# GpSimd's long products in pieces, retention's decay in the addition, and five weight buffers in place of four

## The chip, the cores and the metric

The kernel runs on one core of one Trainium2 chip. What counts is the device time of one execution, in microseconds, as the median of several runs. TensorE (PE in the profile) multiplies matrices, PEld is its loading of weights, VectorE is DVE, ScalarE is ACT, GpSimd is POOL, and SP (SyncE) issues the DMAs.

## What is computed

One inference step of a two-layer decoder trunk of width 2048, for 272 positions of a prompt and 8 sequences of 4 new tokens, 304 columns together. In each layer one input projection feeds four mixers (gated delta, RG-LRU, GLA, retention); their outputs are gated and go through one output projection. The reference, cut to the projections and to retention, whose state update the change touches:

```python
proj = jnp.einsum('bld,de->ble', rms_norm(x, lp['norm']), lp['w_in'])
(qkv_a, alpha_a, beta_a, x_b, q_c, k_c, v_c, r_c, q_d, k_d, v_d, gate) = split_last(proj, IN_SIZES)
...
def step(s, inp):                      # retention, one chunk; S_t = gamma_h S_{t-1} + k_t^T v_t
    qc, kc, vc = inp
    attn = jnp.einsum('bihk,bjhk->bhij', qc, kc) * intra
    o = (jnp.einsum('bihk,hi,bhkv->bihv', qc, from_state, s)
         + jnp.einsum('bhij,bjhv->bihv', attn, vc))
    s_new = s * chunk_decay[:, None, None] + jnp.einsum('bjhk,hj,bjhv->bhkv', kc, to_state, vc)
    return s_new, o
...
mixed = jnp.concatenate([o_a, o_b, o_c, o_d], axis=-1) * jax.nn.silu(gate)
y = x + jnp.einsum('ble,ed->bld', mixed, lp['w_out'])
```

Delta and GLA have the same form of update: the old state times a decay, plus a product of keys and values.

## The kernel before

All activations lie transposed: 128 features in the partitions, the 304 columns in the free dimension. The weights of a projection are cut into units of 4 blocks of 128x128. A unit is loaded by one DMA of 256 KB into a buffer `raw`; ScalarE rounds it to `hi` (a type that TensorE multiplies fast), VectorE subtracts to get the rest `lo` from `raw` and `hi`, and TensorE then does 12 matrix products with it: `hi` with the high and the low part of the activations (`xh`, `xl`), and `lo` with the high part, for each of the 4 blocks. There are 512 units, so 6144 of these products, which the profile lists as `main` (in the start also as `d`). `RB` and `HB` are the numbers of `raw` and of `hi`/`lo` buffers, and they also set how far ahead the steps stand: at the start of unit u the program has `low(u + HB - 2)`, `split(u + HB - 1)` and, behind the second block, `load(u + HB - 2 + RB)`.

Between these products the mixers' small work is woven in. Each mixer is a generator (`delta_thread`, `pair_thread` for GLA with m = "g" and retention with m = "r", `lru_thread`), and a clock model in the program, with a price for each kind of instruction, decides behind which product the next piece of a generator is written. So the order on each engine is fixed when the program is built, and every engine works strictly in its own order. A small product whose input is late on the chip holds up all products behind it. The tag `e` names the PSUM banks of rows, GLA, LRU and retention, `d` those of delta.

The states of the 8 new-token sequences and of the prompt lie in one tile `S9` of 9 blocks of 128x128. A mixer reads the old state with 9 small products (`reads`, whose left side `lxd`, `lxg` or `lxr` is copied together by GpSimd), GpSimd multiplies the state by its decay, and later VectorE adds new products (`advance`). For these GpSimd spreads the values over the sequences (`spread`): 8 blocks in one instruction for delta, twice 4 for GLA and retention. `o_norm` sums squares by two products with ones, whose two inputs are `hq` (ScalarE) and `lq` (VectorE). `zq` and `zk` are the inputs of GLA's level products. The line L302 is that of the helper that records every instruction.

Of the kernel before, what the change touches and what calls it, by code (L numbers as in the profile page):

```python
# [9 lines left out]
F32 = mybir.dt.float32  # L10
# [34 lines left out]


KU = 4
HB = 4
RB = 4
NH = KT // KU  # L50
NW = 16
NN = 20
# [301 lines left out]
def trunk(ctx: ExitStack, tc: tile.TileContext, I, O):  # L354
    nc = tc.nc
    clk = Clocks()
    pe, act, dve, pool, sp = (Engine(e, k, clk) for e, k in ((nc.tensor, "P"), (nc.scalar, "A"), (nc.vector, "V"),
                                                             (nc.gpsimd, "G"), (nc.sync, "S")))
    mul, add, sub = ALU.mult, ALU.add, ALU.subtract
# [17 lines left out]
    def store(out, in_):  # L377
        r = clk.ready
        sp.dma_start(out=out, in_=in_)
        clk.ready = r  # L380
# [30 lines left out]
    def C(name, a=0, n=1):  # L411
        return cst[:, CC[name] + a:CC[name] + a + n]
# [22 lines left out]
    els = one.tile([128, 12], F32, name="els")  # L435
# [110 lines left out]
    def spin(t, tag, n):  # L546
        turn[tag] = (turn.get(tag, -1) + 1) % n
        clk.slot[t.tensor.name] = f"{tag}{turn[tag]}"
        return t
# [15 lines left out]
    def load(u, to=KU):  # L565
# [3 lines left out]
        if u == 0:  # L569
            if u not in raws:  # L570
                raws[u] = spin(wp.tile([128, KU, 128], F32, tag="raw", name="raw", bufs=RB), "raw", RB)
            k = 0 if to < KU else 1
            store(raws[u][:, k:to, :], I["w_in"][l, e - 1][:, k:to, :])
            return
        raws[u] = spin(wp.tile([128, KU, 128], F32, tag="raw", name="raw", bufs=RB), "raw", RB)
        store(raws[u], (I["w_in"][l, e - 1] if ph == "in" else I["w_out"][l, e])[:, KU * q:KU * q + KU, :])

    def split(u):
        if u >= len(units):
            return  # L580
        r = raws.pop(u)
        his[u] = spin(wp.tile([128, KU, 128], F32R, tag="hi", name="hi", bufs=HB), "hi", HB)
        los[u] = spin(wp.tile([128, KU, 128], F32R, tag="lo", name="lo", bufs=HB), "lo", HB)
        for ks in PARTS if u == 0 else (slice(0, KU),):
# [259 lines left out]

    def spread(vm, R, blocks):

        n = blocks.shape[1]
        pool.tensor_mul(vm, R[:, None, 128:256].bitcast(F32).to_broadcast([128, n, 128]),
                        blocks[:, :, None].to_broadcast([128, n, 128]))

    def copies(out, x, n):

# [2 lines left out]
            pool.tensor_copy(out=out[:, 128 * b:128 * b + 16 * n].rearrange("p (u t) -> p u t", u=n),  # L855
                             in_=x[:, None, c:c + 16].to_broadcast([128, n, 16]))

    def advance(tag, S9, p0, n, products):
        ps = pt(tag)
        for i, (out, k, v) in enumerate(products):  # L860
            pe.matmul(ps[out, :128 * n], k, v, start=i == 0 or out.start > 0,
                      stop=i + 1 == len(products) or products[i + 1][0].start > 0)
        dve.tensor_add(S9[:, p0:p0 + n, :], S9[:, p0:p0 + n, :],
                       ps[:, :128 * n].rearrange("p (b v) -> p b v", v=128))

    busy = []

# [31 lines left out]
    def delta_thread(l, p, tag):  # L899
# [4 lines left out]
        K, Q, V, KN, VB, KTL, Eb, AT, qe, egl = ({} for _ in range(10))  # L904
# [16 lines left out]
        for h in range(2):  # L921
            ps = yield from totals(tag, s[h][:, :T])
# [15 lines left out]
        for h in range(2):  # L938
            for src, d, k in ((V, VB, 1), (KN, KTL, 3)):
                d[h] = yield from take(1, src is V)  # L940
                ps = pt(tag)
# [49 lines left out]
        for r in range(2):  # L991
            for u in range(2):
                n = 512 - 16 * u
# [4 lines left out]
        for j in range(15):  # L998
            n, m = 15 - j, j // 2 + 1
# [39 lines left out]
        for h, c, a in hca:  # L1039
            r = slice(32 * a, 32 * a + 32)  # L1040
# [6 lines left out]
        for h, c, a in hca:  # L1047
            r = slice(32 * a, 32 * a + 32)
# [53 lines left out]
        VN, SS, S9 = {}, {}, {}  # L1102
# [7 lines left out]
        ps = pt(tag)  # L1110
# [5 lines left out]
        ps = pt(tag)  # L1116
# [5 lines left out]
        ps = pt(tag)  # L1122
        for h in range(2):
            pe.matmul(ch(ps, h), KN[h][:, 128:256], SS[h][:, 0:128], start=True, stop=True)
        for h in range(2):
            dve.scalar_tensor_tensor(ch(VB[h], 1), ch(ps, h), col[:, 2, 1, hs[h]:hs[h] + 1], ch(VB[h], 1),
                                     op0=mul, op1=add)
        yield
        ps = pt(tag)
# [5 lines left out]
        ps = pt(tag)  # L1135
# [5 lines left out]
        LQ, SL, R = {}, {}, {}  # L1141
# [5 lines left out]
        ps = pt(tag)  # L1147
# [4 lines left out]
        for h in range(2):  # L1152
            R[h], LQ[h] = yield from take(2)
            R[h] = recast(R[h], F32R)
            pk = pt(tag)
            pe.transpose(pk[:, 0:128], KN[h][:, 256:384], ident)
            pool.memset(LQ[h][:, 0:128], 0.0)
            sc = col[:, 3, 2, hs[h]:hs[h] + 1]
            hi_lo(R[h][:, 0:128], pk[:, 0:128], 64, sc)
            activ(LQ[h][0:16, 0:128], pk[0:16, 0:128], AF.Copy, scale=sc[0:16])  # L1160
            spots(lx["d"], 0, slice(0, 128), KN[h])
            spots(lx["d"], 1, slice(0, 128), qe[h])
            give(KN[h])
            yield
            pr = reads(tag, lx["d"], S9[h])
            activ(SL[h][:, 0:128], pr, AF.Copy)
            pool.tensor_mul(S9[h], S9[h], egl[h][:, 2:11, None].to_broadcast([128, 9, 128]))
            yield
        for h in range(2):
            ps = pt(tag)  # L1170
# [6 lines left out]
        for h in range(2):  # L1177
# [4 lines left out]
            ps = pt(tag)  # L1182
# [14 lines left out]
        for h in range(2):  # L1197
            vm = recast((yield from take9()), F32R)
# [84 lines left out]
    def pair_thread(l, p, m, tag):  # L1283
# [23 lines left out]
        S9 = yield from take9()  # L1307
# [44 lines left out]
        if m == "r":  # L1352
            yield from bg.vacant(tag, 2)
            ps2 = [pt(tag), pt(tag)]
            for c, (c0, n) in enumerate(CH):
                for h in range(2):
                    r = slice(64 * h, 64 * h + 64)
# [5 lines left out]
        for h in range(2):  # L1363
            ps = pt(tag)
# [82 lines left out]
        R = yield from take(2)  # L1447
        R = [recast(x, F32R) for x in R]
        ps, ps2 = pt(tag), pt(tag)
# [9 lines left out]
        else:  # L1459
            for h in range(2):  # L1460
                for c in range(2):
                    b = 128 * c + 64 * h
# [4 lines left out]
        for b in range(2):  # L1467
            hm = C("hs", 0, 2)[:, :, None].to_broadcast([128, 2, 64])
            v, k = ps2[:, 128 * b:128 * b + 128], ps2[:, 256 + 128 * b:384 + 128 * b]
# [5 lines left out]
            for h in range(2):  # L1475
                r, own = slice(64 * h + 32, 64 * h + 64), slice(64 * h, 64 * h + 64)
                if sc is None:
                    dve.tensor_sub(R[b][r, own], k[r, own], R[b][r, own].bitcast(F32))
                else:
                    dve.scalar_tensor_tensor(R[b][r, own], k[r, own], sc[r], R[b][r, own].bitcast(F32),  # L1480
                                             op0=mul, op1=sub)
            activ(R[b][:, 128:256], v, AF.Copy)
            dve.scalar_tensor_tensor(R[b][:, 128:256], R[b][:, 128:256].bitcast(F32), C("um", 0), v,
                                     op0=mul, op1=add)
# [7 lines left out]
        ps = pt(tag)  # L1492
        for c in range(2):
            for h in range(2):
                b = 128 * c + 64 * h
# [10 lines left out]
        pr = reads(tag, lx[m], S9)  # L1506
        activ(sel[:, 0:128], pr, AF.Copy)
        if m == "g":
            pool.tensor_mul(S9, S9, els[:, 2:11, None].to_broadcast([128, 9, 128]))
        else:  # L1510
            pool.tensor_scalar(S9[:, 0, :], S9[:, 0, :], C("dec", 3 * p + 1), None, op0=mul)
            pool.tensor_scalar(S9[:, 1:9, :], S9[:, 1:9, :], C("dec", 3 * p + 2), None, op0=mul)
        yield
        sqs_ = yield from take(2)
        yield from bg.vacant(tag, 2)
        ps = [pt(tag), pt(tag)]
        for h in range(2):
            r = slice(64 * h, 64 * h + 64)
# [9 lines left out]
        for h in range(2):  # L1528
# [3 lines left out]
            give(sqs_[h])  # L1532
        give(sel, SS, qe)
        advance(tag, S9, 0, 1, [(slice(64 * h, 64 * h + 64), ktb[:, 64 * h:64 * h + 64], VT[h][0:16, 256:384])
                                for h in range(2)])
        give(*VT)
        vm = recast((yield from take9()), F32R)
        for b in range(2):
            spread(vm[:, 4 * b:4 * b + 4], R[b], C("m4", 0, 4))
        yield  # L1540
        for b in range(2):
            advance(tag, S9, 1 + 4 * b, 4, [(slice(0, 128), R[b][:, 0:128], vm[:, 4 * b:4 * b + 4, :])])
            yield
        give9(recast(vm, F32))
        give(*[recast(x, F32) for x in R])
# [91 lines left out]
    load_x(2, 2)  # L1637
    for u in range(1, RB):
        load(u)
# [9 lines left out]
    for kt in range(KU):  # L1649
        x_split(0, kt, xin[kt])  # L1650
        if kt < HB - 1:
            split(kt)
            if kt < HB - 2:
                low(kt)
                load(kt + RB)
    for kt in range(LAG):
        squares(kt, xin[kt], sqs[kt % 6])

    def begin(u):
        kt = KU + u  # L1660
        if kt < KT:
            x_split(0, kt, xin[kt])
        low(u + HB - 2)
        split(u + HB - 1)
        load(u + HB - 2 + RB)
        for k in range(LAG + u, KT) if kt == KT else (LAG + u,):
# [47 lines left out]
    for u, (l, ph, e, q) in enumerate(units):  # L1714
# [4 lines left out]
        else:  # L1719
            low(u + HB - 2)  # L1720
            split(u + HB - 1)
            if LOADK == 0:
                load(u + HB - 2 + RB)
        if ph == "in" and q == 0:
# [20 lines left out]
        a, b = ([t[:, k, :] for k in range(KT)] for t in (xh, xl)) if ph == "in" else (mh, ml)  # L1745
# [21 lines left out]
        if q == NH - 1:  # L1767
# [4 lines left out]
            kind, i = ORDER[e]  # L1772
# [109 lines left out]
```

## Time and profile before

| what | before |
|---|---|
| median of 3 runs | 1091.02 us (1091.01 to 1096.0) |
| profiled execution: time, span of the instructions | 1089.9 us, 1088.0 us |
| mean granted TensorE clock | 0.991 |
| TensorE products: busy | 1042.6 us, 96% |
| VectorE, ScalarE, GpSimd: busy | 746.0, 639.7, 412.9 us |
| DMA | 186.86 MB, mean 172 GB/s |

The busy time of TensorE counts a product from its start to its modelled end, and products overlap in the pipeline; so the small difference between busy time and span is idle time, while a product that comes late by less than the pipeline's depth does not show as idle. The last TensorE product ends some 9 us before the span's end.

### The profile page before, as it was taken

The numbers are of one execution on the slowest core, as the hardware profiler recorded it, in microseconds if no ns is written. First come the engines' busy times: TensorE is split into PE (matmuls) and PEld (weight loads), VectorE is DVE, ScalarE is ACT, GpSimd is POOL, SyncE is SP. The second block draws the span as 40 slices with busy tenths as digits, with TensorE's granted clock in tenths as the row PEclk, the third lists the DMA queues.
The fourth block names the chain that finished last, engine by engine and source line by source line (L and its number), as shares of the span: only waits on it lengthen the run. The fifth ranks groups of instructions, "written<-read, shape, count | busy, mean of one in ns | idle before, by whom it ended". The sixth has DMA issues, their size and how long they took to land.

```text
span 1088.0 us, 23535 instructions
## 1 busy us (share of the span) xinstructions
PE 1042.6 (96%) x8358; PEld 995.1 (91%) x8358; DVE 746.0 (69%) x1457; ACT 639.7 (59%) x1438; POOL 412.9 (38%) x843
## 2 busy tenths in 40 slices
PE   8999999998999999999999998999999999899995
PEld 7899988988998999999999998888999998899995
DVE  5867588798656467556667757878886576765664
ACT  6677954665745766455455876555765466554542
POOL 4423374534518343022222348344254346211110
PEclk9999999999999999999999999999999999999998
DMA  6555434545465555666644545336545663566563
GB/s 212 188 150 187 134 123 138 189 148 190 139 208 186 174 165 181 198 208 211 206 134 144 178 149 164 126 102 212 178 152 159 201 214 122 176 202 207 184 191 138
DMA packets 116893, 186.86 MB, mean 172 GB/s; under 512 B 22184, under 2 KB 45368, under 8 KB 116776
## 3 DMA queue, kind: packets, MB, share of 16 engines
q1 hardware_dynamic: 116776, 185.37, 53.1%
q8 instruction: 65, 1.06, 0.4%
q14 instruction: 52, 0.43, 0.1%
HBM read 164.10 MB, written 19.96 MB: 169 GB/s over the span
## 4 chain that ended last, share of the span: by engine, by line
PE 67%; DVE 13%; DMA 5%; POOL 5%; issue 5%; ACT 4%; SPq 1%; DVEq 0%; ACTq 0%; POOLq 0%
PE main L302 55%; PE e L302 6%; PE d L302 5%; DMA raw<-in_w_in_dram 4%; DVE lo L302 4%; DVE m L302 2%; DVE n L302 2%; POOL m L302 2%; ACT hi L302 1%; DVE zq L302 1%; DVE acc L302 1%; POOL s9.4_4198 L302 1%; POOL n L302 1%; ACT L369 1%; SPq L302 1%
## 5 line engine op out<-in xcount | busy, mean ns | idle before, releaser
L302 PE MATMUL main<-xh,hi 128*128 128x304 f32 (+2 forms) x1488 | 468.7, 315 | 2.8 <-ACT xh L302 2.5
L302 DVE TENSOR_TENSOR lo<-raw,hi 128x512 fp32r<-128x512 f32 (+1 forms) x513 | 391.7, 782 | 101.6 <-ACT hi L302 100.0
L302 PE MATMUL main<-xh,lo 128*128 128x304 f32 (+2 forms) x1488 | 449.8, 302 | 4.2 <-DVE lo L302 4.2
L302 ACT ACTIVATE hi<-raw 128x512 fp32r<-128x512 f32 (+1 forms) x513 | 316.7, 625 | 228.6 <-PE main L302 95.9
L302 PE MATMUL main<-xl,hi 128*128 128x304 f32 (+2 forms) x1488 | 447.6, 301 | 0.4 <-DVE xl L302 0.3
L302 PEld LDWEIGHTS main<-xh,hi 128*128 128x128 f32 x1488 | 281.8, 189 | 14.8 <-issue 6.8
L302 PEld LDWEIGHTS main<-xh,lo 128*128 128x128 f32 x1488 | 281.6, 189 | 7.3 <-DVE lo L302 7.1
L302 PEld LDWEIGHTS main<-xl,hi 128*128 128x128 f32 x1488 | 282.2, 190 | 2.7 <-DVE xl L302 0.9
L302 PE MATMUL main<-m,hi 128*128 128x304 f32 (+1 forms) x1024 | 208.7, 298 | 0.0
L302 PEld LDWEIGHTS main<-m,hi 128*128 128x128 f32 x1024 | 166.5, 188 | 0.0
L302 PE MATMUL main<-m,lo 128*128 128x304 f32 (+1 forms) x512 | 153.3, 299 | 0.0
L302 POOL TENSOR_TENSOR ssq<-ssq,n 128x304 f32<-128x304 f32 (+1 forms) x29 | 34.8, 1200 | 167.4 <-ACT n L302 167.4
L302 PEld LDWEIGHTS main<-m,lo 128*128 128x128 f32 x512 | 96.1, 188 | 0.0
L302 POOL COPY cvo<-ct 128x3 f32<-128x3 f32 x64 | 31.6, 522 | 136.1 <-DVE ct L302 136.0
L302 POOL TENSOR_TENSOR n<-n,n 128x304 f32<-128x304 f32 (+1 forms) x38 | 35.5, 951 | 113.7 <-ACT n L302 69.1
L302 ACT ACTIVATE n<-n 128x304 f32<-128x304 f32 (+4 forms) x118 | 49.5, 438 | 36.0 <-DVE n L302 26.0
L302 DVE TENSOR_TENSOR n<-main,n 128x304 f32<-128x304 f32 (+1 forms) x32 | 14.9, 466 | 61.3 <-PE main L302 51.8
L369 ACT ACT_TABLE_LOAD x35 | 44.9, 1283 | 0.6
L302 DVE SCALAR_TENSOR_TENSOR acc<-ct,par,acc 128x328 f32<-128x328 f32 x64 | 40.7, 636 | 4.9 <-ACT acc L302 3.8
L302 ACT ACTIVATE m<-m 128x304 f32<-128x304 f32 (+5 forms) x95 | 39.3, 431 | 6.9 <-DVE m L302 3.1
L302 DVE TENSOR_TENSOR n<-main,rstd 128x304 f32<-128x304 f32 (+1 forms) x42 | 19.5, 465 | 26.4 <-PE main L302 26.0
L302 ACT ACTIVATE n<-e 128x304 f32<-128x304 f32 (+5 forms) x67 | 19.6, 307 | 28.9 <-PE e L302 15.4
(416 smaller groups left out, 1334.5 us busy)
## 6 DMA issues: line engine op xcount, KB each, us to landing
raw<-in_w_in_dram SPq DMA_DIRECT2D x383, 256.0 KB
raw<-in_w_out_dram SPq DMA_DIRECT2D x128, 256.0 KB
n<-o_dram SPq DMA_DIRECT2D x28, 152.0 KB
o_dram<-m SPq DMA_DIRECT2D x19, 152.0 KB
m<-in_x_dram SPq DMA_DIRECT2D x16, 152.0 KB
n<-in_x_dram SPq DMA_DIRECT2D x16, 152.0 KB
xs_dram<-n SPq DMA_DIRECT2D x16, 152.0 KB
n<-xs_dram SPq DMA_DIRECT2D x16, 152.0 KB
```

Source lines behind the costliest of these rows:

```text
L302: r = f(*a, **k)
L369: nc.scalar.preload_act_table_set(want[0])
```

## The change

Four things. `spread` multiplies two blocks (256 elements) per instruction, in place of all 4 or 8. The decay of delta's and GLA's states is multiplied in three instructions of three blocks (384 elements), in place of one of nine. Retention's decay on GpSimd is gone; `advance` multiplies by it while it adds, in one VectorE instruction with a scalar. And `HB` and `RB` go from 4 to 5, so that each `split`, `low` and `load` belongs to one unit later, `load` to two units later.

```diff
-HB = 4
-RB = 4
+HB = 5
+RB = 5
...
     def spread(vm, R, blocks):
 
-        n = blocks.shape[1]
-        pool.tensor_mul(vm, R[:, None, 128:256].bitcast(F32).to_broadcast([128, n, 128]),
-                        blocks[:, :, None].to_broadcast([128, n, 128]))
+        for i in range(0, blocks.shape[1], 2):
+            pool.tensor_mul(vm[:, i:i + 2], R[:, None, 128:256].bitcast(F32).to_broadcast([128, 2, 128]),
+                            blocks[:, i:i + 2, None].to_broadcast([128, 2, 128]))
+
+    def decay(S9, by):
+
+        for i in range(0, 9, 3):
+            pool.tensor_mul(S9[:, i:i + 3], S9[:, i:i + 3], by[:, i:i + 3, None].to_broadcast([128, 3, 128]))
...
-    def advance(tag, S9, p0, n, products):
+    def advance(tag, S9, p0, n, products, by=None):
...
-        dve.tensor_add(S9[:, p0:p0 + n, :], S9[:, p0:p0 + n, :],
-                       ps[:, :128 * n].rearrange("p (b v) -> p b v", v=128))
+        o, x = S9[:, p0:p0 + n, :], ps[:, :128 * n].rearrange("p (b v) -> p b v", v=128)
+        if by is None:
+            dve.tensor_add(o, o, x)
+        else:
+            dve.scalar_tensor_tensor(o, o, by, x, op0=mul, op1=add)
...
-            pool.tensor_mul(S9[h], S9[h], egl[h][:, 2:11, None].to_broadcast([128, 9, 128]))
+            decay(S9[h], egl[h][:, 2:11])
...
         if m == "g":
-            pool.tensor_mul(S9, S9, els[:, 2:11, None].to_broadcast([128, 9, 128]))
-        else:
-            pool.tensor_scalar(S9[:, 0, :], S9[:, 0, :], C("dec", 3 * p + 1), None, op0=mul)
-            pool.tensor_scalar(S9[:, 1:9, :], S9[:, 1:9, :], C("dec", 3 * p + 2), None, op0=mul)
+            decay(S9, els[:, 2:11])
```

Since the clock model prices the pieces, the small work also moves between the products. Three places show it.

In the start, on ScalarE's row, before the change: `xh` is an activation block (the inputs `m_112` to `m_114` are blocks 2 to 4), `hi` a unit's rounded weights, and `m_127` to `m_130` and `ssq` are squares for the norm.

```order
L302 ACTIVATE xh<-m_112,par 128x304
L302 ACTIVATE hi<-raw 128x512
L302 ACTIVATE xh<-m_113,par 128x304
L302 ACTIVATE ssq<-m_110 128x304
L302 ACTIVATE m_127<-m_111 128x304
L302 ACTIVATE m_128<-m_112 128x304
L302 ACTIVATE m_129<-m_113 128x304
L302 ACTIVATE xh<-m_114,par 128x304
L302 ACTIVATE hi<-raw 128x512
```

And with the change:

```order
L302 ACTIVATE xh<-m_112,par 128x304
L302 ACTIVATE hi<-raw 128x512
L302 ACTIVATE xh<-m_113,par 128x304
L302 ACTIVATE hi<-raw 128x512
L302 ACTIVATE ssq<-m_110 128x304
L302 ACTIVATE m_127<-m_111 128x304
L302 ACTIVATE m_128<-m_112 128x304
L302 ACTIVATE m_129<-m_113 128x304
L302 ACTIVATE xh<-m_114,par 128x304
L302 ACTIVATE hi<-raw 128x512
```

The rounding of unit 3 stands ahead of four squares and of the fifth activation block; on SP's row the fifth weight load likewise stands ahead of blocks 4 to 11 of the activations.

On GpSimd's row in layer 0, GLA's second pair, before: `zk` are the inputs of its level products, `s9.2_3562` takes delta's spread values, the copies into `lxg` come behind.

```order
L302 TENSOR_TENSOR zk_92<-m_635,g_141 128x76x2
L302 TENSOR_TENSOR n_2991<-n_2991,m_633 128x304
L302 TENSOR_TENSOR zk_91<-n_2992,g_141 128x152
L302 TENSOR_TENSOR s9.2_3562<-n_2950,cst 128x1024
L302 TENSOR_TENSOR g_141<-g_141,n_156 128x304
L302 COPY m_638<-g_141 128x128 x2
```

With the change:

```order
L302 TENSOR_TENSOR zk_92<-m_644,g_141 128x76x2
L302 TENSOR_TENSOR zk_91<-m_645,g_141 128x152
L302 TENSOR_TENSOR g_141<-g_141,n_153 128x304
L302 COPY n_155<-g_141 128x128 x2
...
L302 TENSOR_TENSOR s9.3_171<-s9.3_171,els 128x384 x3
L302 TENSOR_TENSOR s9.2_3709<-n_3058,cst 128x256 x4
```

The delta thread has come later here, and its spread values stand behind GLA's decay, no longer among the level products.

On GpSimd's row near the end of layer 1's mixers, before: the `128x288` rows are the gating products, `g_144` the squares for delta's last norm, and the two long rows the last two spreads.

```order
L302 TENSOR_TENSOR n_154<-n_154,n_4399 128x288
L302 TENSOR_TENSOR n_5487<-n_5487,n_3654 128x288
L302 TENSOR_TENSOR g_144<-g_144,n_156 128x304
L302 TENSOR_TENSOR s9.2_12855<-n_12357,cst 128x1024
L302 TENSOR_TENSOR s9.3_12891<-g_12431,cst 128x1024
```

With the change:

```order
L302 TENSOR_TENSOR n_11602<-n_11602,n_165 128x288
L302 TENSOR_TENSOR n_12601<-n_12601,n_6023 128x288
L302 TENSOR_TENSOR n_11603<-n_11603,n_5279 128x304
L302 TENSOR_TENSOR s9.0_12918<-n_12389,cst 128x256 x4
L302 TENSOR_TENSOR s9.4_12957<-n_12514,cst 128x256 x4
```

Here nothing has moved: the two long rows have become eight short ones at the same place.

## Rows read from the trace of the kernel before

**Rows 1.** The page's first part: busy time, share of span.

```profile
PE 1042.6 (96%) x8358; PEld 995.1 (91%) x8358; DVE 746.0 (69%) x1457; ACT 639.7 (59%) x1438; POOL 412.9 (38%) x843
```

**Rows 2.** TensorE's waits, whole run: total us, times, longest us.

```profile
PE e L302 <- DVE zq L302: 7.8, 9, 2.7
...
PE d L302 <- DVE lq L302: 4.5, 2, 3.0
...
PE main L302 <- DVE lo L302: 4.2, 10, 1.1
...
PE e L302 <- DVE lq L302: 2.2, 2, 1.7
...
PE d L302 <- DVE s9.2_3655 L302: 2.2, 1, 2.2
...
PE d L302 <- DVE lo L302: 1.2, 3, 0.6
...
PE d L302 <- POOL lxd L302: 0.8, 1, 0.8
```

**Rows 3.** A wait of ScalarE, whole run.

```profile
ACT hi L302 <- DMA raw<-in_w_in_dram: 88.8, 65, 5.0
```

**Rows 4.** TensorE's timeline: start, duration, what, [idle before].

```profile
151.84 0.30 PE L302 MATMUL main<-xl,hi 128*128 128x304 f32 x1
...
152.44 0.41 PE L302 MATMUL main<-xh,lo 128*128 128x304 f32 x1 [0.30 <-DVE lo L302]
...
152.69 0.30 PE L302 MATMUL main<-xh,hi 128*128 128x304 f32 x1
...
152.83 0.30 PE L302 MATMUL main<-xl,hi 128*128 128x304 f32 x1
...
247.08 0.52 PE L302 MATMUL e<-zq,zk 128*64 128x64 f32 x10 [2.74 <-DVE zq L302]
```

**Rows 5.** GpSimd's timeline at three places: start, duration, what.

```profile
244.01 1.89 POOL L302 TENSOR_TENSOR s9.2_3562<-n,cst 128x1024 fp32r<-128x1024 f32 x1
...
336.06 0.84 POOL L302 TENSOR_TENSOR n<-n,s9.1_2990 128x304 f32<-128x304 f32 x1
...
933.54 2.36 POOL L302 TENSOR_TENSOR s9.2_12855<-n,cst 128x1024 fp32r<-128x1024 f32 x1
...
935.86 2.11 POOL L302 TENSOR_TENSOR s9.3_12891<-g,cst 128x1024 fp32r<-128x1024 f32 x1
```

**Rows 6.** VectorE's timeline at two of these places.

```profile
335.97 2.28 DVE L302 TENSOR_TENSOR lo<-raw,hi 128x512 fp32r<-128x512 f32 x1
...
934.06 4.22 DVE L302 TENSOR_TENSOR m<-n,m 128x288 fp32r<-128x288 f32 x2
...
938.20 0.68 DVE L302 TENSOR_TENSOR lo<-raw,hi 128x512 fp32r<-128x512 f32 x1
...
938.80 0.46 DVE L302 TENSOR_TENSOR lq<-g,hq 128x304 fp32r<-128x304 f32 x1
```

**Rows 7.** Stretches: us, TensorE busy, granted clock, DMA share, GB/s.

```profile
733.00:739.00 6.00, 5.75 (x40) 1.00 0.48 159
...
747.50:751.50 4.00, 3.73 (x18) 0.57 0.66 214
...
939.50:943.50 4.00, 4.00 (x21) 0.66 0.36 107
```

**Rows 8.** GpSimd's groups by shape: out<-in, count, busy us, mean ns.

```profile
L302 POOL TENSOR_TENSOR s9.1_5407<-n,cst 128x512 fp32r<-128x512 f32 x2 | 2.0, 1046 | 0.0
...
L302 POOL TENSOR_TENSOR s9.0_4398<-s9.0_4398,els 128x1152 f32<-128x1152 f32 x1 | 2.1, 2110 | 0.0
...
L302 POOL TENSOR_SCALAR s9.4_10071<-s9.4_10071,cst 128x1024 f32<-128x1024 f32 x1 | 2.8, 2844 | 0.0
```

**Rows 9.** VectorE's groups by shape.

```profile
L302 DVE TENSOR_TENSOR s9.0_4398<-s9.0_4398,e 128x128 f32<-128x128 f32 x2 | 0.6, 289 | 0.7 <-PE e L302 0.5 <-POOL s9.3_171 L302 0.2
...
L302 DVE SCALAR_TENSOR_TENSOR s9.0_4398<-n,cst,e 128x128 f32<-128x128 f32 x1 | 0.3, 334 | 0.0
```

More of the change, by code (lines that the diff above doesn't have):

```diff
@@ L1534, in pair_thread @@
         advance(tag, S9, 0, 1, [(slice(64 * h, 64 * h + 64), ktb[:, 64 * h:64 * h + 64], VT[h][0:16, 256:384])
-                                for h in range(2)])
+                                for h in range(2)], C("dec", 3 * p + 1) if m == "r" else None)
         give(*VT)
@@ L1541, in pair_thread @@
         for b in range(2):
-            advance(tag, S9, 1 + 4 * b, 4, [(slice(0, 128), R[b][:, 0:128], vm[:, 4 * b:4 * b + 4, :])])
+            advance(tag, S9, 1 + 4 * b, 4, [(slice(0, 128), R[b][:, 0:128], vm[:, 4 * b:4 * b + 4, :])],
+                    C("dec", 3 * p + 2) if m == "r" else None)
             yield
```

## The prediction

> **What bounds the kernel now.** I read the page's first part, then who TensorE waits for, then the timelines around its longest waits. The page says that TensorE's products fill 96% of the span [rows 1]; so a gain can only come out of its idle time, and the reader is to see in [rows 2] what that is made of. Two kinds stand out. The first is waits for `lo`, the rest of a weight unit: 4.2 us in 10 waits in `main` and 1.2 us in 3 in `d`. The second is waits for small VectorE results: `zq` 7.8 us with one of 2.7, `lq` in `d` 4.5 us in 2 (so 3.0 and 1.5), `lq` in `e` with one of 1.7, and one addition to a state, 2.2 us. Of VectorE itself the reader is to see that such a result is late because of GpSimd: two subtractions of the gate take 4.22 us together from 934.06, where the next instructions of similar size take 0.68 and 0.46 us alone [rows 6]; meanwhile GpSimd runs two products of 1024 elements from 933.54 to 935.90 and from 935.86 to 937.97 [rows 5]. The pair ends at 938.28, 0.3 us behind the second product. So an instruction of VectorE that meets a GpSimd product waits until that ends. The third thing to see is that ScalarE waits 88.8 us, in 65 waits, for the weights' DMA [rows 3]: in stretches the loading of a unit is late, and `hi` and `lo` with it.
>
> An idle time costs more than its row says. At 152.44 the row says 0.30 us, but the product starts 0.60 us behind the one before it, where undisturbed ones follow each other every 0.14 us (152.69 and 152.83) [rows 4]; of the 0.46 us lost 0.16 us comes on top of the wait, for filling the pipeline again. And behind two of the waits, that for the state's addition and that of 3.0 us for `lq`, the granted clock falls: 0.57 and 0.66 over 4.00 us [rows 7], part of it at 1.2 in place of 2.4 GHz, which loses 0.43 and 0.34 of 4 us, 1.7 and 1.4 us.
>
> **Weights a unit further ahead.** The work is the same; only the lead grows. `lo` was made ready two units (24 products, 24 x 0.14 = 3.4 us) before its use and is now three (5.0 us); a load had three units between its issue and the rounding and has four. Every wait for `lo` is shorter than one unit's 1.7 us (the longest is 1.1 [rows 2]). So all 13 could go: 5.4 us idle and 13 x 0.16 = 2.1 us, 7.5 us in all. From below it is 0: a wait that goes takes no work away from VectorE, which then is as late for the next small product as it was for `lo`. The four waits of the start are not of that sort, since nothing small stands there yet: rounding and loads come earlier in the row, ahead of squares and of activation blocks that are needed only later; their share is 1.5 us (the 1.2 of `d` and 0.3 of `main`) and 4 x 0.16, 2.1 us. Of the other 5.4 I take 3.4, since in that part most of them come where the DMA is late and VectorE is not. **Taken: 5.5 us, between 0 and 7.5.**
>
> **GpSimd's products in pieces.** A piece is not in the trace. From 1046 ns for 512 elements and 2110 for 1152 [rows 8] the slope is 1064/640 = 1.66 ns an element and the fixed part 0.2 us; so 256 elements take 0.62 us and 384 take 0.83 us. Eight blocks in 4 pieces then take 2.48 us in place of 1.89 [rows 5], a decay in 3 pieces 2.5 in place of 2.11. What VectorE waits for is one piece, no longer the whole. For this to help VectorE must get in between two pieces that stand back to back, and [rows 5, 6] show it twice: the first subtraction from 934.06 runs between the product ending at 935.90 and the next one, which stretches from 1.89 to 2.11 us.
>
> At the 939 wait nothing moves but the cut, so it can be followed. GpSimd's first piece begins when the `lo` before it is done, about 934.05. First subtraction: waits for piece 1 until 934.55, runs 0.45, ends 935.0. Piece 2 to 935.6, second subtraction to 935.95; piece 3 to 936.5, `lo` to 937.1; piece 4 to 937.65, `lq` to 938.0. Before, `lq` ended at 939.26 [rows 6]: 1.3 us of the 3.0 idle are won, and with 1.7 us idle I expect the clock to stay up, as it did behind the 1.7 us wait for `lq` in `e` (1.00 from 733 to 739 [rows 7]), another 1.4. That is 2.7 us. At the 2.7 us wait of `zq` at 247.08 [rows 4] the product of 1024 at 244.01 [rows 5] stood among the level products and has moved behind them; I take the whole wait, 2.7 + 0.16 = 2.9. The other three (1.5, 1.7 and 2.2 us, and the clock behind the last, 1.7, and 3 x 0.16 = 7.6 us) get the share of the first site without its clock, 1.3 of 3.0, and so 3.3, less 0.4 since one of them stood behind products of 512 that shrink less: 2.9. **Taken: 2.7 + 2.9 + 2.9 = 8.5 us. Bounds: all five waits gone, 11.1 + 0.8 + 3.1 = 15 us; and nothing, if VectorE doesn't get in.**
>
> **Retention's decay in the addition.** Four times a scalar product of 1024 elements on GpSimd, 2844 ns [rows 8], and a small one of 128 go away, over 11.4 us; against that the pieces cost 12 decays x 0.4 + 8 x 0.6 + 16 spreads of 512 x 0.2 = 12.8. GpSimd's total stays as it was, and with 38% busy it bounds nothing; what it delays is priced as a rival. On VectorE the combined form takes 334 ns where the plain addition takes 289 at 128x128 [rows 9]; 12 of them cost 0.5 us, beside TensorE's products and behind the last use of the state, where only its store waits. Nothing on the path.
>
> **What the new order costs.** The small work stands at other places, and some of the places will be bad. Here nothing can be read off; I take 2 us, one wait like the largest that are left, between 0 and 8, near half of the 17.5 us that [rows 2] lists for small work.
>
> **The sum:** 5.5 + 8.5 - 2 = 12 us. From the profiled execution's 1089.9 us that is 1077.9; the median of the runs is 1.1 us above it, so **1079 us**, with 1074 to 1085 as this case's own range.
>
> **The skill against the trace.** The rows show VectorE stopped by GpSimd for up to a whole product. The Trainium skill (SBUF — State Buffer, "Who interferes with whom") says that a VectorE instruction with two SBUF inputs and a GpSimd instruction that reads SBUF exclude each other over their whole length, and that the one that starts first wins. That speaks against the change as well: each cut is also a place at which VectorE stops GpSimd. The stretched second product (2.11 for 1.89) agrees. The rival on the slower side is what this would come to.
>
> **The rivals.** *VectorE doesn't get in.* At 335.97 `lo` took 2.28 us, 1.6 more than alone, and passed not only the product of 0.84 us at 336.06 but an equal one right behind it [rows 5, 6]: it was shut out over both. If it goes so with pieces, VectorE waits for all of them, 0.6 us longer than now at the four sites that remain; then the products give 2.9 - 2.4 = 0.5, and the sum is 5.5 + 0.5 - 2 = 4 us: **1087**, no change that counts.
>
> *The waits only change place.* VectorE is 69% busy [rows 1] and as late as before, and the new order makes almost as many waits as it removes: 14 less 12, **1089**. For it speaks that the order is a model's that knows nothing of waits between VectorE and GpSimd; against it that the longest waits have a cause that the cut removes at its own place.
>
> *Slower.* The chain over a decay becomes longer. Behind the first head's decay stand, on GpSimd's row, the copies into `lxd` of the second, for which TensorE waits (0.8 us once now [rows 2]). Each of the two inner cuts lets in a VectorE instruction of 0.68 us: 2.5 + 1.4 = 3.9 us in place of 2.11. If that comes out at the 8 delta heads, 8 x (1.8 + 0.16) = 15.7 us, and the clock falls twice more, 3.1: 18.8 - 12 = 7 us slower, **1098**. It decides from about 6 of the 8 heads (6 x 1.96 = 12). Against it: the model prices the pieces longer too, and writes the reads later.
>
> *More.* All `lo` waits and most of the long ones go: 7.5 + 15 - 2 = 20.5, **1070**.
>
> **How the numbers follow.** Forecast 0.57, more 0.10, shut out 0.14, change of place 0.11, slower 0.08. A measurement here can tell about 0.5%, 5.5 us, from no change. Faster by that is nearly all of the forecast (0.55), the larger case and the better edge of the shut-out one (0.05): 0.70. Within it: the rest of these and the change of place, 0.22. Slower: 0.08. The range leaves out the slower case and part of the larger one: 1068 to 1092.
>
> **What would show it.** Right: waits for `lo` under 1.5 us in TensorE's list; no VectorE instruction over 1.5 us beside a GpSimd piece; the wait for `lq` near the end of layer 1's mixers at 1.5 to 2 us with the clock at 1.00 behind it; pieces of 0.6 and 0.8 us; ScalarE's waits for weights well under 88.8 us. Wrong: VectorE rows of 2 us beside several pieces, new waits for `lxd` or `zk` of over 1 us, or TensorE's idle time as large as before under other names.

## The result and the profile after

The changed kernel takes 1076.7 us in the median of 6 runs (1073.1 to 1078.6), the kernel before beside it 1093.5 (1090.0 to 1097.5): a ratio of 0.985, 95% interval 0.982 to 0.988, 16.8 us less by the medians. These 6 runs of the kernel before lie high: 69 other runs of it have a median of 1091.3 us, and from that the gain is 14.6 us (a ratio of 0.9866). The forecast was 1079, range 1068 to 1092. The profiled execution took 1076.1 us with a span of 1073.8.

The page's first part, against [rows 1]:

```profile
PE 1037.2 (97%) x8358; PEld 994.6 (93%) x8358; DVE 736.4 (69%) x1457; ACT 643.7 (60%) x1440; POOL 420.4 (39%) x899
```

TensorE does the same work in a span 14 us shorter. GpSimd has 56 instructions more and 7.5 us more to do. TensorE's longest waits now, against [rows 2]:

```profile
PE e L302 <- DVE zq L302: 7.0, 8, 2.1
PE main L302 <- ACT xh L302: 2.5, 2, 2.1
PE main L302 <- DVE xl L302: 2.3, 4, 1.1
PE d L302 <- DVE g L302: 2.1, 1, 2.1
PE d L302 <- DVE lq L302: 1.8, 3, 1.3
...
PE e L302 <- DVE s9.3_10206 L302: 1.2, 1, 1.2
...
PE e L302 <- DVE lq L302: 0.9, 1, 0.9
```

No wait for `lo` is left, where there were 13 with 5.4 us, and those for `lq` have come down from 6.7 to 2.7 us. Those for `zq` have hardly changed. At the start the waits for `lo` (1.6 us of the 5.4) have become waits for `xl`, 2.3 us where before had 0.3. All rows of this view sum to 25.6 us, before to 33.8; so 8.2 of the 14 us are waits that the view lists. Another 5.4 are busy time (1042.6 to 1037.2), which also counts stretches of lower clock (granted 0.991 on average before, 0.993 now) and lateness under the pipeline's depth. And ScalarE's row, against [rows 3]:

```profile
ACT hi L302 <- PE main L302: 140.5, 164, 2.6
...
ACT hi L302 <- DMA raw<-in_w_in_dram: 23.0, 18, 3.4
```

`hi` waits 23 us for weights, not 88.8, and 140 us, before 95.9, for TensorE to free a split buffer: the load is late 18 times, not 65. For the weights of the output projections it waited 22.4 us in 17 waits before; now the view lists none.

The place that the prediction followed step by step, the end of layer 1's mixers, against [rows 5] and [rows 6]; first VectorE's timeline, then GpSimd's, then TensorE's (start, duration, what, idle before):

```profile
919.95 1.10 DVE L302 TENSOR_TENSOR lo<-raw,hi 128x512 fp32r<-128x512 f32 x1 [2.24 <-ACT hi L302]
920.97 1.65 DVE L302 TENSOR_TENSOR m<-n,m 128x288 fp32r<-128x288 f32 x2
922.54 1.10 DVE L302 TENSOR_TENSOR lo<-raw,hi 128x512 fp32r<-128x512 f32 x1
923.56 0.88 DVE L302 TENSOR_TENSOR lq<-n,hq 128x304 fp32r<-128x304 f32 x1
```

```profile
920.45 3.66 POOL L302 TENSOR_TENSOR s9.0_12918<-n,cst 128x256 fp32r<-128x256 f32 x4
924.07 1.99 POOL L302 TENSOR_TENSOR s9.4_12957<-n,cst 128x256 fp32r<-128x256 f32 x3
```

```profile
924.50 0.41 PE L302 MATMUL d<-lq,onesr 128*128 128x304 f32 x1 [1.28 <-DVE lq L302]
```

The two subtractions `m` take 1.65 us together in place of 4.22, and `lo` and `lq` wait one piece each. The engines alternate, so the four pieces take 3.66 us in place of 2.36 for the whole product; that time is GpSimd's, and nobody waits for it. TensorE waits 1.28 us for `lq` where it waited 3.0, and the granted clock behind it, against the third of [rows 7], stays up:

```profile
923.50:927.50 4.00, 3.00 (x22) 3.00 (x23) 3.11 (x6) 2.44 (x5) 3.58 (x5) 1.00 0.41 126
927.50:931.50 4.00, 4.00 (x30) 3.83 (x29) 3.32 (x6) 1.26 (x2) 0.00 (x0) 1.00 0.45 144
```

(Busy us of PE, PEld, DVE, ACT, POOL, then the granted clock, the DMA share and GB/s.) GpSimd's pieces where nothing disturbs them, and the state's update on VectorE with the decay (first) and without it:

```profile
L302 POOL TENSOR_TENSOR s9.0_11372<-m,cst 128x256 fp32r<-128x256 f32 x4 | 2.3, 613 | 0.0
L302 POOL TENSOR_TENSOR s9.4_4111<-s9.4_4111,egl 128x384 f32<-128x384 f32 x3 | 2.4, 828 | 0.8 <-PE d L302 0.8
```

```profile
L302 DVE SCALAR_TENSOR_TENSOR s9.4_4111<-s9.4_4111,cst,e 128x512 f32<-128x512 f32 x2 | 1.5, 748 | 0.8 <-PE e L302 0.6
L302 DVE TENSOR_TENSOR s9.4_172<-s9.4_172,d 128x512 f32<-128x512 f32 x2 | 1.3, 684 | 2.4 <-PE d L302 2.4
```

Counted by the same `main` product in both traces (the 2304th and the 5376th of 6144, with which the output projections begin), the changed kernel is 6.6 us ahead at the end of layer 0's mixers and 15.9 at the end of layer 1's, and gives back 1.7 in the last projection.

### The profile page after: what moved, and what is told of

Same layout as the page of the kernel before. It is cut to its first block, busy times and chain, and to the rows that moved or that the text cites. A ratio compares the mean times of both kernels' runs of the same rounds, so it can differ in the third digit from the quotient of the medians.

```text
span 1073.8 us, 23604 instructions
## 1 busy us (share of the span) xinstructions
PE 1037.2 (97%) x8358; PEld 994.6 (93%) x8358; DVE 736.4 (69%) x1457; ACT 643.7 (60%) x1440; POOL 420.4 (39%) x899
## 4 chain that ended last, share of the span: by engine, by line
PE 75%; DVE 12%; DMA 4%; issue 3%; POOL 2%; ACT 2%; SPq 1%; DVEq 0%; ACTq 0%; POOLq 0%
PE main L302 62%; PE e L302 7%; PE d L302 7%; DVE lo L302 4%; DVE n L302 2%; DVE m L302 2%; DMA raw<-in_w_in_dram 2%; DVE zq L302 1%; POOL s9.3_171 L302 1%; DVE acc L302 1%; ACT hi L302 1%; SPq L302 1%; DVE xl L302 1%; DMA s9.1_169<-in_w_lru_dram 1%; DMA s9.0_11449<-in_ret_dram 1%
## 5 line engine op out<-in xcount | busy, mean ns | idle before, releaser
L302 DVE TENSOR_TENSOR lo<-raw,hi 128x512 fp32r<-128x512 f32 (+1 forms) x513 | 387.1, 775 | 86.1 <-ACT hi L302 83.1
L302 ACT ACTIVATE m<-m 128x304 f32<-128x304 f32 (+8 forms) x95 | 39.2, 430 | 7.9 <-DVE m L302 3.8
```

Of the source, the lines that this page charges most:

```text
L302: r = f(*a, **k)
```

## The experiments

The theory is the prediction's: the lead removes TensorE's waits for `lo`, the pieces let VectorE in, retention's decay does nothing, and the new order costs a little. The rivals: all of it comes from one part alone; or from the order, which each part changes. Ratios are to the kernel before on the same chip, 6 runs of each kernel (12 of those within 0.5% of it) against 23, for the changed kernel 6 against 6. The 23 have medians of 1091.2 to 1091.5 on either chip, the 6 beside the changed kernel 1093.5; so where its 0.985 is set against another row, the same with 0.9866 is given too. What a ratio is in us is worked out by 1091.5. In the table "order" is that of which kernel, where an experiment holds it; "own" is what the planner makes of the parts, so that two rows with "own" differ in their order too. The last columns are TensorE's waits for `lo` and ScalarE's for `raw` from `w_in`, in each profile (us, times).

| raw, split | products | retention's decay | order | ratio (95%) | `lo` | `raw` |
|---|---|---|---|---|---|---|
| 4, 4 | whole | GpSimd | (before) | 1 | 5.4, 13 | 88.8, 65 |
| 4, 4 | whole | addition | own | 0.9967 (0.9953 to 0.9981) | 8.3, 19 | 90.0, 68 |
| 4, 4 | whole | GpSimd | pieces alone | 0.9997 (0.9983 to 1.0011) | 7.4, 17 | 81.4, 62 |
| 4, 4 | pieces | GpSimd | own (pieces alone) | 0.9963 (0.9947 to 0.9980) | 6.9, 15 | 80.2, 61 |
| 4, 4 | pieces | GpSimd | before | 0.9926 (0.9908 to 0.9945) | 6.4, 13 | 78.4, 57 |
| 4, 4 | pieces | addition | own | 0.9967 (0.9951 to 0.9983) | 6.8, 14 | 77.2, 55 |
| 4, 5 | pieces | addition | own | 0.9976 (0.9959 to 0.9993) | 1.0, 2 | 82.8, 62 |
| 5, 4 | pieces | addition | own | 0.9905 (0.9884 to 0.9926) | 2.9, 8 | 26.0, 20 |
| 5, 5 | whole | GpSimd | own | 0.9972 (0.9954 to 0.9989) | none | 21.8, 16 |
| 5, 5 | whole | addition | after | 0.9907 (0.9886 to 0.9928) | none | 22.9, 20 |
| 5, 5 | pieces | GpSimd | own | 0.9885 (0.9859 to 0.9911) | none | 28.9, 21 |
| 5, 5 | pieces | addition | planned as whole | 0.9943 (0.9924 to 0.9962) | none | 20.6, 17 |
| 5, 5 | pieces | addition | (after) | 0.985 (0.982 to 0.988) | none | 23.0, 18 |

**The lead alone.**

```diff
-HB = 4
-RB = 4
+HB = 5
+RB = 5
```

> Only the five raw and five split buffers; GpSimd's products whole, retention's decay on GpSimd. The result to be split is 16.8 us (1093.5 to 1076.7). By the prediction's terms the lead brings 5.5 us of the 12 to 17: about 1088, with no wait of TensorE for lo left and ScalarE's 88.8 us of waits for raw falling to near the 23 us that the changed kernel has, while the waits for lq and zq stay at about 7 and 8 us and the clock still falls twice in mid-run. Rival, all from the lead: about 1077. Rival, a wait for lo only becomes another wait of VectorE: 1093, no lo waits but the idle time of TensorE as large as before under other names.

0.9972, 3.1 us: between the 5.5 of the theory and nothing, far from all of it. The waits for `lo` are gone and those for `raw` are down, as expected, but TensorE's waits for VectorE's small results rose:

```profile
PE e L302 <- DVE zq L302: 9.8, 9, 2.1
...
PE d L302 <- DVE lq L302: 3.4, 3, 2.7
PE e L302 <- DVE lq L302: 3.1, 3, 1.7
PE d L302 <- DVE g L302: 2.7, 1, 2.7
```

All rows of this view whose releaser is VectorE, without `lo` and `xl`, sum to 23.4 us, before to 17.1. The mean granted clock of its runs was lower too, 0.986 where the kernel before had 0.989. So with whole products the last rival, waits that change place, took most of the lead's gain, in this order.

**The pieces alone, in their own order,** and **in the order of before**: the latter charges each group of pieces to the planner as one product, which leaves every engine's row as it was.

```diff
+        for i in range(0, n, 2):
+            nc.gpsimd.tensor_mul(vm[:, i:i + 2], ...)
+        clk.op("G", price("G", "tensor_mul", 128 * n, vm, 0), [vm], [R, blocks])
```

> Only GpSimd's products in pieces, with the order that follows from their prices; four buffers, retention's decay on GpSimd. By the prediction's terms pieces bring 8.5 us less up to 2 for the new order: 1085 to 1087; the waits for lo stay (about 5 us in 13 waits), and no wait of TensorE for lq of over 1.5 us is left, since VectorE gets in between two pieces. Rival, all from the lead: 1093. Rival, VectorE is shut out over all pieces: 1093 or more, with VectorE instructions of 2 us and more beside pieces of 128 rows.

> The pieces run, but the planner charges them as one whole product, so that every engine's row stands as in the kernel before, with each long product of GpSimd replaced by its pieces in the same place. This is the cut with no new order. If the cut itself does it: the 3.0 us wait for lq near 939 shrinks to about 1.7 and the clock stays up behind it, other waits behind a product by 1.3 us each, together 5 to 8 us faster than before: 1086 to 1089. If the pieces help only by what stands elsewhere in the new order: 1093 or, since 1024 elements in pieces take 0.6 us longer and a decay 0.4 longer, slower than before, up to 1096.

0.9963 and 0.9926, 4.0 and 8.1 us. With the order held the cut alone gives what was expected of it, and where it was expected. TensorE's wait near the end of layer 1, in this run:

```profile
936.75 0.41 PE L302 MATMUL d<-lq,onesr 128*128 128x304 f32 x1 [1.30 <-DVE lq L302]
```

1.3 us, not 3.0; the waits for small VectorE results, summed as above, are 8.8 us, before 17.1. The order made for pieces then costs 4.0 of the 8.1 us.

**Whole products in the order of the changed kernel, and in that of the pieces alone:** the planner is charged for pieces, and one long product runs.

```diff
+        nc.gpsimd.tensor_mul(vm, R[...].to_broadcast([128, n, 128]), blocks[...])
+        for i in range(0, n, 2):
+            clk.op("G", price("G", "tensor_mul", 256, vm, 0), [vm], [R, blocks])
```

> The order of the changed kernel on every engine, with its buffers and retention's decay in the addition, but each group of pieces runs as the one long product it was. It tells the cut apart from the order and the lead. If the cut is worth the 8.5 us of the prediction: about 1085, with waits of 2 us and more for small results behind products of 1 to 2 us. If the gain comes from the lead and the new order: 1077, no slower than the changed kernel.

> The mirror of the pieces in the order of before: whole products of the kernel before in the order that the planner makes for pieces, four buffers, retention's decay on GpSimd. So only the order differs from before, and only the cut from the run with pieces alone (0.9963). If the cut is worth 0.6 to 0.7% in every order (0.74% in that of before, 0.57% in that of the changed kernel): ratio 1.002 to 1.004, slower than before, with the small VectorE waits of TensorE 3 to 6 us above those of the run with pieces. If the cut is only worth what the order makes of it: 0.996, as with the pieces.

0.9907, between the two expected values: to take the cut back in this order costs 0.57%, 6.2 us (0.9907 less 0.985, of 1091.5), or 4.5 us by 0.9866. The place at the end of layer 1 is as it was before, on VectorE, on TensorE, and in the granted clock behind it:

```profile
922.42 4.22 DVE L302 TENSOR_TENSOR m<-n,m 128x288 fp32r<-128x288 f32 x2
```

```profile
927.68 0.62 PE L302 MATMUL d<-lq,onesr 128*128 128x304 f32 x1 [3.02 <-DVE lq L302]
```

```profile
927.50:931.50 4.00, 3.82 (x16) 3.82 (x17) 2.23 (x5) 1.58 (x3) 0.00 (x0) 0.50 0.26 77
```

4.22 and 3.0 us, with the clock at its lower level (0.50 of 2.4 is 1.2 GHz) for the whole of the next 4 us. The other order with whole products gave 0.9997, not the slower time expected: there the cut is worth 0.34%, 3.7 us. So it gains in all three orders, and how much depends on what the order puts beside it.

**Retention's decay alone, pieces with it, and everything but it.** The first has only the `by` of `advance` and no scalar products on GpSimd; the second is the changed kernel with four buffers; the third is the changed kernel with the scalar products back.

```diff
-HB = 5
-RB = 5
+HB = 4
+RB = 4
```

```diff
+        else:
+            pool.tensor_scalar(S9[:, 0, :], S9[:, 0, :], C("dec", 3 * p + 1), None, op0=mul)
+            pool.tensor_scalar(S9[:, 1:9, :], S9[:, 1:9, :], C("dec", 3 * p + 2), None, op0=mul)
```

> Only retention's decay in the addition; four buffers, whole products. The lead alone brought 0.3%, pieces alone 0.4%, and the changed kernel 1.5%, so 0.8% (9 us) stand in neither. If they are retention's decay itself, this is 1083 to 1085 beside 1093.5 of before (or 0.8% faster on this chip). By the prediction's term, nothing on the path, it is within 0.3% of before, with TensorE's idle time only shifted by the new order.

> The changed kernel with four raw and four split buffers. If the lead is worth what it was alone, 0.3%: ratio to before 0.988. If the lead is what the pieces need (VectorE late for lo again), and the parts only pay together: 0.993 or more. By the prediction's 5.5 us: 0.990.

> The changed kernel with retention's decay still two scalar products of GpSimd (2.8 us and a small one, four times). If that decay costs nothing on the path: ratio to before as the changed kernel's, 0.985, within 0.003 of it by the chances of another order. If it is the missing 9 us: 0.993. If lead and pieces just add: 0.993 too; then the retention run tells which of the two.

0.9967, 0.9967 and 0.9885. Added to the kernel before, retention's decay brings 0.33%, added to the pieces nothing (0.9963 to 0.9967), and added to lead and pieces 0.35%, or 0.2% by 0.9866 (0.9885 to 0.985, intervals overlapping). So it is not the missing 9 us. Some 5 of them are in lead and pieces together: 0.9885 where the two apart would add up to 0.9935. The other 2 to 4 us, from 0.9885 to 0.9866 or 0.985, are no more than another order does.

**The changed kernel in another order:** its pieces charged to the planner as whole products.

> The changed kernel, but the planner charges each group of pieces as one whole product, so the order is the one of whole products and the pieces stand in it. In the order of before the pieces brought 0.74%, in the order that follows from their own prices 0.37%; so by that the new order cost 0.37%, 4 us. If charging them dearer makes a worse order in general: this is faster than the changed kernel, about 0.981. If it was chance of one order: 0.985 give or take 0.004, with no direction.

0.9943 against 0.985: the same instructions, the same buffers and 10 us slower (8 by 0.9866), by the order alone. In the order of before it had gone the other way by 4 us. So the direction that was expected is refuted: to plan the pieces at their own prices cost 4.0 us with four buffers (0.9926 to 0.9963) and gained 8 to 10 us with five. What an order is worth follows no rule that these runs show.

**Which buffer.** The changed kernel with one of the two numbers at 4.

```diff
-HB = 5
-RB = 5
+HB = 5
+RB = 4
```

> The changed kernel with five split buffers and four raw ones: split a unit further ahead, the load stands as many units before the rounding as in the kernel before. If the lead of the split is what removed the waits for lo (11 us of lost time in TensorE's row before, under 1 in the changed kernel): lo waits stay under 2 us and ratio 0.985 to 0.989; ScalarE's waits for raw stay near 89 us. If the load was what was late: lo waits of 5 us or more, and 0.993.

> The changed kernel with four split buffers and five raw ones: only the load is a unit further ahead. If the lead of the split is what counts: waits for lo as without any lead (over 8 us of lost time, ratio 0.993 to 0.997, the same as with four and four), while ScalarE's waits for raw fall to near 23 us. If the load was what was late: lo waits under 3 us and 0.985 to 0.989.

Five split and four raw buffers: 0.9976, with 1.0 us of waits for `lo` left. Four split and five raw: 0.9905, with 2.9. Neither expectation came whole: the split's lead removes the waits for `lo`, as said, and yet no time with four raw buffers (0.9967 to 0.9976). The raw buffer leaves some of these waits and brings 0.62% (0.9967 to 0.9905), 6.8 us, without the other. With five raw buffers the fifth split buffer does bring time: 0.9905 to 0.985 or 0.9866, 4 to 6 us. But each of these four kernels has its own order, so each step holds what its order is worth as well. ScalarE's waits for `raw`, of these two kernels:

```profile
ACT hi L302 <- DMA raw<-in_w_in_dram: 82.8, 62, 4.1
```

```profile
ACT hi L302 <- DMA raw<-in_w_in_dram: 26.0, 20, 3.5
```

All seven kernels of the table with four raw buffers have 77 to 90 us of this wait and ratios of 0.9926 to 1 (mean 0.9971); the six with five have 21 to 29 us and 0.985 to 0.9972 (mean 0.9910). In the chain of work that ended last, on each kernel's page, this DMA has 3 to 5% of the span in the seven and at most 2% in the six (none with the lead alone, whose chain covers only three quarters of the span).

**Memsets over all rows.** This one asks about a thing that the traces showed (the last section), in the order of the changed kernel.

```diff
-        pool.memset(XB[64:128, 0:192], 0.0)
+        pool.memset(XB[:, 0:192], 0.0)
...
-        pool.memset(X6[0:64, 0:256], 0.0)
+        pool.memset(X6[:, 0:256], 0.0)
```

> The changed kernel in its own order; only two memsets of GpSimd on 64 of 128 partitions (64x192 and 64x256) are made over all 128 partitions, at the same places. In the changed kernel's trace the subtraction m at 356.36 and a lo at 851.17 started beside a 64-row memset and were shut out over it and over the products behind it (2.71 and 2.29 us, 4 pieces and 2 products of 304). If the part of the partitions is what lets the next GpSimd instruction in without a gap: both come down to 1.1 us or less, TensorE's wait for lq near 359 (0.9 us) goes or halves, and the time falls by 1 to 3 us (0.997 to 0.999 of the changed kernel's, hardly to be told). If it is the memset itself or chance: the same two instructions still take over 2 us.

0.9872 (0.9850 to 0.9895): not faster, and not to be told from the changed kernel's 0.985 to 0.9866. No version measured here is faster than the changed kernel. What it says of its question stands in the last section.

## Why the prediction was right

The time was within 2.3 us of the forecast, and inside the case's own range; the gain was 15 to 17 us where 12 were forecast. The steps one by one:

- **VectorE gets in between two pieces:** right. At the followed place the sequence came out as written, `lq` 0.4 us earlier still (idle 1.28 us, forecast 1.7), and the clock stayed at 1.00. Not everywhere: one sign of being wrong showed once, a VectorE row of 2.71 us beside four pieces (the last section). The piece times, worked out at 0.62 and 0.83 us, are 0.613 and 0.828.
- **The pieces' size, 8.5 us:** somewhat too high; with the order held they gave 8.1, 4.5 to 6.2, and 3.7 us. Of the 2.9 us for the wait of `zq` at 247 some 1.8 came: the waits for `zq` of that stretch sum to 4.1 us before (230 to 251) and 2.3 after (238 to 246). The other three waits of the step, 1.5, 1.7 and 2.2 us, of which it took 43%, are at most 0.3 us each at the same products; but new ones of 1.2 to 2.1 us stand at other places. `zq` still costs 7.0 us in all, with one of 2.1, at 167. No long product makes that one: on VectorE's row two scans and a `lo` stand ahead of the copies that `zq` needs, and some 0.5 us of the scans' 2.03 are a product of GpSimd of 0.58 us beside the second (one such scan alone takes 0.79; VectorE's timeline, then GpSimd's):

```profile
162.33 2.03 DVE L302 TENSOR_TENSOR_SCAN m<-m,m 128x304 f32<-128x304 f32 x2
164.28 0.66 DVE L302 TENSOR_TENSOR lo<-raw,hi 128x512 fp32r<-128x512 f32 x1
164.87 1.59 DVE L302 COPY_PREDICATED m<-levm,e 64x64 f32<-64x64 uint8 x6
166.35 0.63 DVE L302 TENSOR_TENSOR zq<-n,m 64x152 f32<-64x152 f32 x2
167.01 0.79 DVE L302 TENSOR_TENSOR_SCAN m<-m,m 128x304 f32<-128x304 f32 x1
```

```profile
163.14 0.58 POOL L302 TENSOR_TENSOR zk<-n,g 128x152 f32<-128x152 f32 x1
```

- **The lead, 5.5 us:** the size is in the range of what was measured (3.1 us with whole products, 8.5 with pieces, 11.0 to 12.8 with pieces and retention's decay, each in its own order: the ratios' differences by 1091.5), but the reason was the lesser one. The step counted waits for `lo`. These are what the split buffer removes, and alone it brought nothing; the load's extra unit brought 6.8 us without the other, and it shortens ScalarE's waits, which the prediction read [rows 3] and priced only by `lo`. The 2.1 us of the start did not come whole: `xl` is waited for there instead, and at the 220th product, behind the start, the changed kernel is 0.7 us ahead. What stands on ScalarE's row behind a late `hi` starts late too; in the trace of before two `n` stand behind such a wait of 2.16 us, and run as soon as `hi` lets them:

```profile
870.30 0.63 ACT L302 ACTIVATE hi<-raw 128x512 fp32r<-128x512 f32 x1 [2.16 <-DMA raw<-in_w_in_dram]
870.83 0.76 ACT L302 ACTIVATE n<-n 128x288 f32<-128x288 f32 x2
```

That the raw buffer brings time was tried, in each kernel's own order; that it does so by such activations was not, and is only argued: TensorE's list has no wait between 868 and 880 in that trace, so this one cost nothing that shows.
- **Lead and pieces in separate terms:** wrong as a sum. Apart they bring 3.1 and 4.0 us, together 12.6 (0.9885). TensorE's waits for small VectorE results fit the rival of waits that change place: the lead takes them from 17.1 to 23.4 us with whole products, and with pieces leaves them at 14 (14.1 to 13.8). But whole products with the lead in the changed kernel's order have 16.6 us, so the order has its part, and how much of the 5.5 us is whose is not shown.
- **Retention's decay, nothing on the path:** right within what orders do; 0.33%, nothing and 0.2 to 0.35% in three kernels.
- **The new order, 2 us:** right that it is a term, wrong to give it a sign. It cost 4.0 us in one pair, 0.3 us less than nothing in another, and the order of the changed kernel is 8 to 10 us better than that of the same parts planned as whole products. In this the forecast had luck: an order as bad as that one would have left 1084 to 1085 us, at the edge of the case's own range. Lead and pieces together measured 12.6 us, their own order's cost included, where 14 less 2 were forecast; the step to the third part, with its new order, brought 2 to 4 us more instead of nothing.
- **Slower, by the longer chain over a decay:** it did not come; no wait for `lxd` is left in TensorE's list.

## What to carry to other kernels

When two engines shut each other out, cut the long instruction of the one that nobody waits for; read the gain at one place where nothing else moves, and hold the rest of the order to measure it. Ask which buffer is late, by the wait of the engine that first uses the load, not by the last wait in the chain. Where every edit reshuffles a planned order, the order alone can be worth as much as the edits (here 0.3, 4 and 8 to 10 us in 1090): measure an edit in more than one order before believing its sign.

## What the runs showed of the hardware

**Who gets in behind GpSimd.** In the 14 profiles 1,213 VectorE instructions were delayed by over 0.15 us while GpSimd's row ran on without a gap. By which GpSimd end the instruction's undisturbed time, counted back from its own end, starts at, 1,121 got in behind the one that they met, and 92 only behind a later one. (With the undisturbed time set by the fastest tenth of each shape it is 1,134 and 84.) Of the 92, 71 had met a GpSimd instruction on fewer than 128 partitions, where only one of 72 got in at once. Two of the 92 are shown, one in the changed kernel and one in that with memsets over all rows (each VectorE first, then GpSimd):

```profile
356.36 3.10 DVE L302 TENSOR_TENSOR m<-n,m 128x304 fp32r<-128x304 f32 x2
```

```profile
356.14 0.31 POOL L302 MEMSET m<- 64x256 f32 x1
356.42 2.32 POOL L302 TENSOR_TENSOR s9.1_5221<-n,cst 128x256 fp32r<-128x256 f32 x4
```

```profile
353.76 3.08 DVE L302 TENSOR_TENSOR lo<-raw,hi 128x512 fp32r<-128x512 f32 x1 [0.18 <-ACT hi L302]
```

```profile
353.69 0.31 POOL L302 MEMSET m<- 128x256 f32 x1
353.97 2.33 POOL L302 TENSOR_TENSOR s9.1_5221<-n,cst 128x256 fp32r<-128x256 f32 x4
```

The instruction starts beside a memset and is then shut out over all four pieces behind it, which the cut was to prevent (the two `m` take 3.10 us; the same two, undisturbed, 0.85 in the second kernel). The Trainium skill (SBUF — State Buffer, "Who interferes with whom") says that GpSimd instructions which only write SBUF don't contend, and that the first to start holds the lock; by it the `lo` of the second kernel, begun beside a memset and 0.21 us ahead of the first piece (353.76 and 353.97), should have stopped the pieces, and the trace, in which it ends only behind the fourth, disagrees with that as far as the rows' starts tell the order. (For `m` at 356.36 they don't: VectorE's instruction before it ends at 356.44, 0.02 us behind the start of the first piece.) It was expected that a memset on part of the partitions does it. With all 128 rows the `m` of this place ran undisturbed but the `lo` ahead of it took 3.08 us, and the `lo` near 851 took 0.68, though VectorE's row stood otherwise there (it began 0.46 us ahead of the next product). So the part of the partitions is not the cause, or not alone. What is stays open.

**The clock's falls come and go.** Of 69 runs of the kernel before, the eleven at a mean granted clock of 0.986 took 1093.0 us on average and the eight at 0.991 1089.4. How long the clock is at its lower level differs between executions of one kernel, so the falls of one profile are no sure term of a sum.

**The last projection runs at two speeds.** Its products of 288 columns follow each other every 0.132 us in three of the 14 profiles (before, the pieces in its order, and five split with four raw buffers) and every 0.134 us in the others, at a granted clock of 1.00; over 768 products that is the 1.7 us given back. TensorE's timeline of before, then of after (the start of each second `lo` row is three products later):

```profile
1000.00 0.30 PE L302 MATMUL main<-m,lo 128*128 128x288 f32 x1
...
1000.39 0.29 PE L302 MATMUL main<-m,lo 128*128 128x288 f32 x1
```

```profile
1000.22 0.29 PE L302 MATMUL main<-m,lo 128*128 128x288 f32 x1
...
1000.62 0.30 PE L302 MATMUL main<-m,lo 128*128 128x288 f32 x1
```

Nothing in the traces says why.
